# Splitting the weights in the DMA: high parts rounded by the load, low parts by a second, adding transfer

## The chip, the cores and the metric

The kernel runs on one core of a Trainium2 chip. TensorE (PE) multiplies, ScalarE (ACT) and VectorE (DVE) do the elementwise work, SyncE (SP) issues nearly all transfers, and GpSimd (POOL) has nothing to do but a few constants at the start. The metric is the device time of one execution in microseconds. Before the change three runs gave 1938.77, 1940.85 and 1942.29 us, a median of 1940.85 us.

## The reference

Two token streams share the weights: 128 context tokens and 512 latent tokens, 1024 channels each. Two layers follow each other. Layer 0 mixes tokens with a bidirectional state-space scan (the kernel calls it ssd), layer 1 with differential attention (att). Each is followed by a feed-forward block (ffn) with an up-projection, a depthwise convolution of width 3 and a down-projection:

```python
def conv_ffn(h, up_w, conv_w, conv_b, down_w):
    u = dwconv(h @ up_w, conv_w, conv_b)
    a, v = jnp.split(u, 2, axis=-1)
    return (jax.nn.silu(a) * v) @ down_w
...
        xp = xp + p_g1 * op
        xs = xs + s_g1 * os_
        ...
        xp = xp + p_g2 * conv_ffn(modulate(xp, norm_ffn_g[i], p_sh2, p_sc2), *ffn_p)
        xs = xs + s_g2 * conv_ffn(modulate(xs, norm_ffn_g[i], s_sh2, s_sc2), *ffn_p)
```

`modulate` is an RMS norm with a scale and a shift that come from a conditioning vector times a large matrix (`mod_w`). All inputs are float32, and the dense products are wanted at more than one reduced-precision pass gives.

## The kernel before, in words

Activations lie transposed: 128 channels on the partitions, 640 tokens along the row, 512 latent ones first. Every dense product is made in a split form. A float32 weight w is written as a high part (`whi`, rounded to the reduced type float32r) and a low part (`wlo` = w - whi, rounded to the same type), an activation likewise, and three products are summed: high by high, high by low, low by high. Each product is made in two matmuls of 256 and 384 tokens.

Weights are cut into 230 units. A unit is a tile of 128 partitions by up to 1024 columns, that is 8 blocks of 128x128 and 512 KB; it costs PE 8 x 3 x 2 = 48 matmuls. Units are numbered in the order of use: 0 is `w_dt`, 1 to 40 `w_in` (ssd), 41 to 56 `w_so`, 57 to 124 the first ffn (`w_up`, `w_dn`), then `w_qkv`, `w_ao` and the second ffn. `weight_units` lists them.

Three functions carry them. `prefetch` loads a unit into a raw tile (4 buffers) from SP's queue. `cast` makes the high part from the raw tile on ACT (line 134, a copy that rounds) and the low part on DVE (line 135, a subtraction); high and low have 3 buffers each, and in the two ffn stages two more of each for 2 units out of 5 (line 131). `nextw` hands out a unit, and keeps loads three units ahead of use and splits one unit ahead in program order (lines 141 and 142). A raw buffer comes free when DVE has subtracted from it, a high or low buffer when PE has read it for the last time.

The order of instructions on each engine is set by a scheduler from priorities and its own idea of durations. It may move a split further ahead than program order. At run time every engine and every queue works its list strictly in order, so an instruction that waits holds up all behind it. A queue also waits, before it issues a DMA, for the one eight issues earlier on it.

Beside the weights other things are loaded by SP: at the start the tokens (`xT`), constants and four blocks of the first modulation matrix (`modp`; tiles `mp`), later more of it (`mr`), and during the first ffn the second layer's modulation matrix in 48 tiles of 512 KB (`modT`; tiles `mw`, two buffers), which DVE reduces two instructions a tile (line 500). `hook`, called after each block of channels, advances such side tasks.

In the trace the up-projection's PSUM tiles are `up` (the first three of a stage `st`), the projections back to 1024 channels `po`, those of the ssd stage `in`, `x`, `bc`, `z`, those of attention `q`, `k`, `v`; `sl` are attention scores and `e` their exponentials; `uraw` is a copy of an `up` tile that ACT makes.

Of the kernel before, what the change touches and what calls it, by code (L numbers as in the profile page):

```python
# [9 lines left out]
F32 = mybir.dt.float32  # L10
F32R = mybir.dt.float32r
BF16 = mybir.dt.bfloat16
I32 = mybir.dt.int32
AF = mybir.ActivationFunctionType
ALU = mybir.AluOpType
# [3 lines left out]
P = 128  # L19
# [17 lines left out]
SUB = ((0, 8), (8, 15), (15, 22))  # L37
DA_SCALE = 64 ** -0.5
LAM_INIT = 0.8 - 0.6 * math.exp(-0.3 * 1)
RAW = 4  # L40
ATT_SPLIT = 6
NF = 19
RSQRT_MAGIC = float(0x5F3759DF)
# [2 lines left out]
class Step:  # L46
# [68 lines left out]


    def prefetch(self, upto):
        while len(self.wraw) <= min(upto, len(self.units) - 1):
            u = len(self.wraw)
            ap, n = self.units[u]  # L120
            r = self.pw.tile([P, 1024], F32, tag="raw", name=f"raw{u}", bufs=RAW)
            self.nc.sync.dma_start(r[:, :n], ap)
            self.wraw[u] = r

    def cast(self, upto):
        while len(self.wcast) <= min(upto, len(self.units) - 1):
            u = len(self.wcast)
            self.prefetch(u)
            n = self.units[u][1]
            r = self.wraw[u]  # L130
            wp, t, b = (self.pw, "w", 3) if self.px is None or u % 5 < 3 else (self.px, "x", 2)
            hi = wp.tile([P, 1024], F32R, tag=t + "hi", name=f"whi{u}", bufs=b)
            lo = wp.tile([P, 1024], F32R, tag=t + "lo", name=f"wlo{u}", bufs=b)
            self.act(hi[:, :n], r[:, :n], AF.Copy)
            self.tt(lo[:, :n], r[:, :n], hi[:, :n].bitcast(F32), ALU.subtract)
            self.wcast[u] = (hi, lo)

    def nextw(self):
        u = self.wi
        self.wi += 1  # L140
        self.prefetch(u + 3)
        self.cast(u + 1)
        return self.wcast[u]

    def dense(self, ps, w, ks, h):
# [332 lines left out]
    def mod_rest(self, l, t0, pool):  # L478


        nc, a = self.nc, self.a
        cb = pool.tile([P, 2, D], F32, tag="cbc", name="cbc", bufs=1)
        nc.sync.dma_start(cb, a["cbc"])
        for c in range(2):
            sb = self.pw.tile([P, 1024], F32, tag="raw", name="csil", bufs=RAW)
            self.act(sb, cb[:, c, :], AF.Tanh, scale=0.5)
            self.stt(cb[:, c, :], sb, 1.0, cb[:, c, :], ALU.add, ALU.mult)
            nc.vector.tensor_scalar(cb[:, c, :], cb[:, c, :], 0.5, None, ALU.mult)
        yield 4
        for t in range(t0 - 1, 48):  # L490
            if t < 47:
                nxt = pool.tile([P, 1024], F32, tag="mw", name="mw", bufs=2)
                nc.sync.dma_start(nxt, a["modT"][t + 1])
            if t < t0:
                w = nxt
                yield 8
                continue
            junk = self.slot("sq", "junk", BF16, cols=1024, bufs=1)
            for c in range(2):
                nc.vector.tensor_tensor_reduce(w if c else junk, w, cb[:, c, :], 1.0, 0.0, ALU.mult, ALU.add,  # L500
                                               self.mod[l][:, t, c:c + 1])
                yield 2 if self.down else 7
            if t % KT == KT - 1:
                for c in range(2):
                    mv = self.mod[l][:, t - KT + 1:t + 1, c]
                    self.tt(mv, mv, self.modb[:, 48 * l + t - KT + 1:48 * l + t + 1], ALU.add)
                if t // KT in (1, 4):
                    self.make_gs(l, t // KT // 3)
            w = nxt
# [590 lines left out]
    def run(self):  # L1100
        tc, nc, a = self.tc, self.nc, self.a
        self.units = self.weight_units()
        self.x = []

        def norm(l, s, h):
            def mk(hf):
                if hf == "A":
                    h.extend(self.new_h(f"h{l}{s}"))
                return self.norm_task(hf, self.gs[l][s], self.shift(l, s), h)
            return mk  # L1110

        hs = [[] for _ in range(4)]
        with tc.tile_pool(name="ssd", bufs=1) as pool:
            self.ssd(hs[0], norm(0, 1, hs[1]), pool)
        with tc.tile_pool(name="ffn0", bufs=1) as pool:
            self.px = pool
            self.modtask = self.add(self.mod_rest(1, 0, pool), 48)
            self.ffn(0, hs[1], norm(1, 0, hs[2]), pool)
            self.px = None
        with tc.tile_pool(name="att", bufs=1) as pool:  # L1120
            self.att_consts(pool)
            self.attention(hs[2], norm(1, 1, hs[3]), pool)
        with tc.tile_pool(name="ffn1", bufs=1) as pool:
            self.px = pool
            self.modtask = None
            self.ffn(1, hs[3], self.final_task, pool)
            for t in reversed(list(self.tasks)):
                self.drain(t)
# [100 lines left out]
```

## Time and profile before

| | |
|---|---|
| median of 3 runs | 1940.85 us (1938.77 to 1942.29) |
| the profiled execution's own time | 1941.6 us |
| its span, first to last instruction | 1939.8 us |
| granted TensorE clock, mean | 0.992 |
| instructions in the span | 33400 |
| bytes moved by DMA | 184.99 MB |

The span is what the profile covers; 1.8 us of the profiled execution lie around it. Busy times are unions of instruction records. Matmuls are pipelined and their ends modelled, so "PE busy" means that some matmul was in flight, not that PE ran at its peak. In the window table each engine has its busy time and its number of instructions, then come the granted clock, the mean busy share of the 16 DMA engines and the rate in GB/s. The chain of waits follows the work that ended last back to the start; a time on it for an engine other than PE is time in which PE's next matmul was held by that engine, or at least released by it last.

### The profile page before, as it was taken

How to read it: one execution, taken by the hardware profiler on the slowest of the kernel's cores; microseconds unless marked ns; L12 is line 12 of the kernel's file. 1: busy time of each engine (PE TensorE's matmuls, PEld its weight loads, DVE VectorE, ACT ScalarE, POOL GpSimd, SP SyncE). 2: the span in 40 equal slices, each digit the busy share in tenths (PEclk: the TensorE clock that was granted, in tenths of full speed). 3: DMA queues.
4: the chain of work that ended last, by engine and by line, in shares of the span. 5: the costliest groups of instructions: out<-in, count | busy, mean ns of one | idle time of the engine just before them, and what ended most of it. 6: DMA issues, size and time to landing. Idle time of an engine off the chain costs nothing.

```text
span 1939.8 us, 33400 instructions
## 1 busy us (share of the span) xinstructions
PE 1892.0 (98%) x13613; PEld 1785.8 (92%) x13613; DVE 1397.2 (72%) x2681; ACT 967.6 (50%) x1789; POOL 0.2 (0%) x4
## 2 busy tenths in 40 slices
PE   7999999999999999999999999999999999999997
PEld 4888888898988999999999988889899999999997
DVE  4779898888948999984455778888877553553554
ACT  2468585868633542243243576666645441441441
POOL 0000000000000000000000000000000000000000
PEclk8999999999999999999999999999999999999998
DMA  9611212113562456632222211111032222222211
GB/s 336 226 59 58 72 47 71 50 66 92 159 211 75 156 181 198 210 119 73 78 68 84 66 45 49 49 46 40 14 114 88 71 72 77 74 69 87 71 39 55
DMA packets 66729, 184.99 MB, mean 95 GB/s; under 512 B 8336, under 2 KB 14736, under 8 KB 66448
## 3 DMA queue, kind: packets, MB, share of 16 engines
q1 hardware_dynamic: 66000, 182.34, 29.1%
q8 instruction: 107, 1.75, 0.4%
q10 hardware_dynamic: 576, 0.52, 0.1%
q14 instruction: 46, 0.38, 0.1%
HBM read 177.06 MB, written 5.77 MB: 94 GB/s over the span
## 4 chain that ended last, share of the span: by engine, by line
PE 92%; ACT 3%; DVE 2%; DMA 1%; issue 1%; SPq 0%; DVEq 0%; ACTq 0%
PE up L102 30%; PE po L102 24%; PE z L102 6%; PE x L102 5%; PE st L102 4%; PE bc L102 3%; PE yp L102 3%; PE k L102 3%; PE q L102 3%; PE v L102 2%; PE sl L102 2%; PE ov L102 1%; PE modrow L102 1%; PE in L102 1%; PE wt L1007 1%; ACT e L93 1%
## 5 line engine op out<-in xcount | busy, mean ns | idle before, releaser
L93 ACT ACTIVATE whi<-raw 128x1024 fp32r<-128x1024 f32 (+4 forms) x230 | 236.1, 1027 | 410.0 <-PE po L102 232.3
L99 DVE TENSOR_TENSOR wlo<-raw,whi 128x1024 fp32r<-128x1024 f32 (+4 forms) x230 | 270.0, 1175 | 183.6 <-ACT whi L93 182.7
L96 DVE SCALAR_TENSOR_TENSOR xr<-po,mod,xr 128x256 f32<-128x256 f32 (+2 forms) x231 | 89.5, 433 | 162.3 <-PE po L102 162.1
L102 PE MATMUL po<-mh,whi 128*128 128x256 f32 (+1 forms) x704 | 167.6, 310 | 0.0
L102 PE MATMUL po<-ml,whi 128*128 128x256 f32 (+1 forms) x704 | 167.3, 310 | 0.0
L102 PE MATMUL po<-mh,wlo 128*128 128x256 f32 (+1 forms) x704 | 167.1, 309 | 0.0
L102 PE MATMUL up<-h01h,whi 128*128 128x256 f32 (+1 forms) x656 | 149.4, 308 | 0.7 <-ACT uraw L93 0.7
L102 PE MATMUL up<-h01h,wlo 128*128 128x256 f32 (+1 forms) x656 | 149.4, 308 | 0.0
L102 PE MATMUL up<-h11l,whi 128*128 128x256 f32 (+1 forms) x656 | 149.3, 308 | 0.0
L102 PE MATMUL up<-h11h,whi 128*128 128x256 f32 (+1 forms) x656 | 149.3, 308 | 0.0
L102 PE MATMUL up<-h11h,wlo 128*128 128x256 f32 (+1 forms) x656 | 149.3, 309 | 0.0
L102 PE MATMUL up<-h01l,whi 128*128 128x256 f32 (+1 forms) x656 | 149.3, 308 | 0.0
L102 PEld LDWEIGHTS po<-mh,whi 128*128 128x128 f32 x704 | 128.4, 188 | 0.6 <-ACT mh L93 0.4
L102 PEld LDWEIGHTS po<-mh,wlo 128*128 128x128 f32 x704 | 128.6, 188 | 0.0
L102 PEld LDWEIGHTS po<-ml,whi 128*128 128x128 f32 x704 | 128.4, 188 | 0.0
L102 PEld LDWEIGHTS up<-h01h,whi 128*128 128x128 f32 x656 | 119.2, 188 | 1.0 <-ACT uraw L93 1.0
L102 PEld LDWEIGHTS up<-h11h,wlo 128*128 128x128 f32 x656 | 119.3, 188 | 0.0
L102 PEld LDWEIGHTS up<-h11l,whi 128*128 128x128 f32 x656 | 119.3, 188 | 0.0
L102 PEld LDWEIGHTS up<-h01h,wlo 128*128 128x128 f32 x656 | 119.2, 188 | 0.0
L102 PEld LDWEIGHTS up<-h11h,whi 128*128 128x128 f32 x656 | 119.2, 188 | 0.0
L102 PEld LDWEIGHTS up<-h01l,whi 128*128 128x128 f32 x656 | 119.2, 188 | 0.0
L96 DVE SCALAR_TENSOR_TENSOR ca<-uraw,fcw,ca 128x127 f32<-128x127 f32 (+1 forms) x176 | 85.3, 545 | 11.4 <-ACT ca L93 11.4
(498 smaller groups left out, 4509.9 us busy)
## 6 DMA issues: line engine op xcount, KB each, us to landing
raw<-in_w_up SPq DMA_DIRECT2D x88, 512.0 KB, 3.5
mw<-in_modT SPq DMA_DIRECT2D x48, 512.0 KB, 3.6
raw<-in_w_in SPq DMA_DIRECT2D x40, 512.0 KB, 3.5
raw<-in_w_dn SPq DMA_DIRECT2D x32, 448.0 KB, 3.3
raw<-in_w_qkv SPq DMA_DIRECT2D x24, 512.0 KB, 3.5
mr<-in_mod SPq DMA_DIRECT2D x44, 256.0 KB, 5.0
raw<-in_w_so SPq DMA_DIRECT2D x16, 512.0 KB, 4.3
raw<-in_w_dn SPq DMA_DIRECT2D x16, 512.0 KB, 3.7
```

The source lines that it names most:

```text
L93: return self.nc.scalar.activation(out, in_, func, **k)
L96: return self.nc.vector.scalar_tensor_tensor(out, in0, s, in1, op0, op1)
L99: return self.nc.vector.tensor_tensor(out, a, b, op)
L102: return self.nc.tensor.matmul(out, lhsT, rhs, start=start, stop=stop)
L1007: nc.tensor.transpose(pm[:, b * P:(b + 1) * P], ws[b][:, kc * P:(kc + 1) * P], self.ident)
```

## The change

The changed kernel does not subtract on DVE. From unit 4 on:

- `prefetch` loads the unit straight into a high tile (float32r, 5 buffers) with a DMA from GpSimd's queue; the DMA converts float32 to float32r as it moves the bytes.
- `cast` lets ACT write the negated high part into the low tile (4 buffers), and then issues a second DMA from GpSimd's queue that reads the same weights again from memory and adds them to what stands in the low tile.
- The raw tiles remain for units 0 to 3 alone (4 buffers in the ssd stage's own pool), which are split on ACT and DVE as before.
- Splits are two units ahead of use in program order instead of one. The extra buffers of the ffn stages are gone.
- Two scratch tiles of the modulation (`csil`) use the `mw` tag instead of a raw buffer, and the descriptor ring for GpSimd's DMAs is 1024 bytes per partition instead of 256.

```diff
-RAW = 4
+FIRST = 4
...
     def prefetch(self, upto):
+
         while len(self.wraw) <= min(upto, len(self.units) - 1):
             u = len(self.wraw)
             ap, n = self.units[u]
-            r = self.pw.tile([P, 1024], F32, tag="raw", name=f"raw{u}", bufs=RAW)
-            self.nc.sync.dma_start(r[:, :n], ap)
+            if u < FIRST:
+                r = self.px.tile([P, 1024], F32, tag="raw", name=f"raw{u}", bufs=FIRST)
+                self.nc.sync.dma_start(r[:, :n], ap)
+            else:
+                r = self.pw.tile([P, 1024], F32R, tag="whi", name=f"whi{u}", bufs=5)
+                self.nc.gpsimd.dma_start(r[:, :n], ap)
             self.wraw[u] = r
 
     def cast(self, upto):
+
         while len(self.wcast) <= min(upto, len(self.units) - 1):
             u = len(self.wcast)
             self.prefetch(u)
-            n = self.units[u][1]
-            r = self.wraw[u]
-            wp, t, b = (self.pw, "w", 3) if self.px is None or u % 5 < 3 else (self.px, "x", 2)
-            hi = wp.tile([P, 1024], F32R, tag=t + "hi", name=f"whi{u}", bufs=b)
-            lo = wp.tile([P, 1024], F32R, tag=t + "lo", name=f"wlo{u}", bufs=b)
-            self.act(hi[:, :n], r[:, :n], AF.Copy)
-            self.tt(lo[:, :n], r[:, :n], hi[:, :n].bitcast(F32), ALU.subtract)
+            ap, n = self.units[u]
+            hi = self.wraw[u]
+            lo = self.pw.tile([P, 1024], F32R, tag="wlo", name=f"wlo{u}", bufs=4)
+            if u < FIRST:
+                r, hi = hi, self.pw.tile([P, 1024], F32R, tag="whi", name=f"whi{u}", bufs=5)
+                self.act(hi[:, :n], r[:, :n], AF.Copy)
+                self.tt(lo[:, :n], r[:, :n], hi[:, :n].bitcast(F32), ALU.subtract)
+            else:
+                self.act(lo[:, :n], hi[:, :n].bitcast(F32), AF.Copy, scale=-1.0)
+                self.nc.gpsimd.dma_start(lo[:, :n], ap, accum_op=ALU.add)
             self.wcast[u] = (hi, lo)
 
     def nextw(self):
         u = self.wi
         self.wi += 1
         self.prefetch(u + 3)
-        self.cast(u + 1)
+        self.cast(u + 2)
         return self.wcast[u]
...
-            sb = self.pw.tile([P, 1024], F32, tag="raw", name="csil", bufs=RAW)
+            sb = pool.tile([P, 1024], F32, tag="mw", name="csil", bufs=2)
...
-    nc = bacc.Bacc("TRN2", target_bir_lowering=False, num_devices=1, dynamic_dma_scratch_size=256)
+    nc = bacc.Bacc("TRN2", target_bir_lowering=False, num_devices=1, dynamic_dma_scratch_size=1024)
```

At the start of the program, on GpSimd's queue after the change (`whi4` is the high tile of unit 4): the loads of units 4 and 5 have nothing before them and no wait.

```order
L127 DMA whi4_447<-in_w_in 128x1024
L127 DMA whi5_449<-in_w_in 128x1024
L127 DMA whi6_708<-in_w_in 128x1024
L144 DMA wlo4_710<-in_w_in 128x1024
L144 DMA wlo5_713<-in_w_in 128x1024
L127 DMA whi7_827<-in_w_in 128x1024
```

Before, the same two units stood on SP's queue behind the tokens, the constants and the loads of all four modulation blocks; so two loads of 512 KB have moved to the front.

In the first ffn's up-projection, SP's queue before the change: the raw loads alternate with the modulation loads.

```order
L122 DMA raw70_7838<-in_w_up 128x1024
L493 DMA mw_8130<-in_modT 128x1024
L122 DMA raw71_7899<-in_w_up 128x1024
L493 DMA mw_8228<-in_modT 128x1024
L122 DMA raw72_7975<-in_w_up 128x1024
```

At the same place on GpSimd's queue after the change; the modulation loads stay on SP, alone.

```order
L127 DMA whi70_7777<-in_w_up 128x1024
L144 DMA wlo69_7779<-in_w_up 128x1024
L127 DMA whi71_7837<-in_w_up 128x1024
L144 DMA wlo70_7839<-in_w_up 128x1024
L127 DMA whi72_7912<-in_w_up 128x1024
L144 DMA wlo71_7914<-in_w_up 128x1024
```

One load per unit has become two, and each adding transfer stands directly behind the high load of the next unit.

On ACT at that place before the change (`up_7699` is the PSUM tile of unit 65, `up_7761` of unit 66): the rounding copy of unit 71 stands ahead of the evacuation of unit 66.

```order
L93 ACTIVATE uraw_7759<-up_7699 128x640
L93 ACTIVATE whi70_7977<-raw70_7838 128x1024
L93 ACTIVATE ca_7819<-uraw_7759,fcw0_7058 128x640
L93 ACTIVATE ca_7819<-ca_7819 128x640
L93 ACTIVATE whi71_8038<-raw71_7899 128x1024
L93 ACTIVATE uraw_7817<-up_7761 128x640
```

And after it (`up_7836` is unit 68): the negation of unit 72 follows the evacuation of unit 68.

```order
L93 ACTIVATE uraw_7834<-up_7776 128x640
L93 ACTIVATE wlo71_7914<-whi71_7837 128x1024
L93 ACTIVATE ca_7893<-uraw_7834,fcw0_7007 128x640
L93 ACTIVATE ca_7893<-ca_7893 128x640
L93 ACTIVATE uraw_7891<-up_7836 128x640
L93 ACTIVATE wlo72_7974<-whi72_7912 128x1024
```

ACT still has one 128x1024 instruction per unit, now later by about two units against PE, and it now waits for a landed high part instead of a landed raw tile.

More of the change, by code (lines that the diff above doesn't have):

```diff
@@ L1113, in run @@
         with tc.tile_pool(name="ssd", bufs=1) as pool:
+            self.px = pool
             self.ssd(hs[0], norm(0, 1, hs[1]), pool)
         with tc.tile_pool(name="ffn0", bufs=1) as pool:
-            self.px = pool
             self.modtask = self.add(self.mod_rest(1, 0, pool), 48)
             self.ffn(0, hs[1], norm(1, 0, hs[2]), pool)
-            self.px = None
         with tc.tile_pool(name="att", bufs=1) as pool:
@@ L1123, in run @@
         with tc.tile_pool(name="ffn1", bufs=1) as pool:
-            self.px = pool
             self.modtask = None
```

## The prediction

> **What bounds the kernel now.** I read the page's first and fourth part, then the table by stretches, then the waits of PE, then single tiles.
>
> ```profile
> PE 1892.0 (98%) x13613; PEld 1785.8 (92%) x13613; DVE 1397.2 (72%) x2681; ACT 967.6 (50%) x1789; POOL 0.2 (0%) x4
> PE 92%; ACT 3%; DVE 2%; DMA 1%; issue 1%; SPq 0%; DVEq 0%; ACTq 0%
> ```
>
> PE has matmuls in flight for 98% of the span and carries 92% of the chain. Only 47.8 us (1939.8 - 1892.0) are free of matmuls, so a change that gives PE nothing less to do has little to win.
>
> ```profile
> 0.00:30.00 30.00, 19.99 (x221) 8.43 (x222) 13.18 (x27) 10.06 (x16) 0.20 (x4) 0.89 0.97 354
> 120.00:240.00 120.00, 119.57 (x932) 106.25 (x930) 106.55 (x212) 85.89 (x214) 0.00 (x0) 1.00 0.18 62
> 240.00:350.00 110.00, 108.42 (x869) 96.41 (x868) 97.55 (x196) 78.14 (x194) 0.00 (x0) 1.00 0.19 63
> 636.00:741.00 105.00, 105.00 (x717) 105.00 (x716) 104.04 (x179) 52.62 (x66) 0.00 (x0) 1.00 0.53 174
> 741.00:797.00 56.00, 56.00 (x391) 56.00 (x390) 55.57 (x100) 11.76 (x13) 0.00 (x0) 1.00 0.70 214
> 797.00:895.00 98.00, 98.00 (x669) 98.00 (x668) 77.62 (x133) 42.37 (x54) 0.00 (x0) 1.00 0.42 128
> 1090.00:1175.00 85.00, 79.02 (x492) 72.30 (x491) 71.32 (x149) 58.00 (x118) 0.00 (x0) 0.98 0.14 43
> 1175.00:1380.00 205.00, 198.80 (x1309) 182.40 (x1308) 172.50 (x341) 139.98 (x286) 0.00 (x0) 1.00 0.14 45
> 1380.00:1457.00 77.00, 73.15 (x537) 68.13 (x536) 56.57 (x126) 36.36 (x66) 0.00 (x0) 1.00 0.25 78
> 1477.00:1583.00 106.00, 106.00 (x725) 106.00 (x724) 64.67 (x100) 53.81 (x66) 0.00 (x0) 1.00 0.27 85
> 1583.00:1639.00 56.00, 56.00 (x384) 56.00 (x383) 20.68 (x35) 10.43 (x12) 0.00 (x0) 1.00 0.23 76
> 1639.00:1738.00 99.00, 99.00 (x677) 99.00 (x676) 52.72 (x81) 44.09 (x54) 0.00 (x0) 1.00 0.23 70
> ```
>
> After length and busy times come clock, DMA share and GB/s. Four things are to be seen. The start is bound by transfers: 354 GB/s with the DMA engines 97% busy. In both ffn blocks (rows from 636 and from 1477) PE is never idle, although DVE is full in the first (104.04 of 105) and half empty in the second: the DVE time of the split costs nothing there. Attention (rows from 1090 to 1457) has 6.0 + 6.2 + 3.85 = 16.0 us without matmuls, the ssd stage 0.4 and 1.6 us in its two rows. And the first ffn already moves twice the bytes of the second, since `modT` is loaded beside the weights.
>
> ```profile
> PE sl L102 <- ACT e L93: 6.6, 7, 2.1
> PE q L102 <- ACT e L93: 5.6, 6, 1.1
> PE po L102 <- DVE wlo L99: 0.6, 1, 0.6
> ```
>
> These are PE's waits (total, times, longest). 12.2 us of attention's 16.0 wait for ACT's exponentials, and the subtraction on DVE, which the change takes away, holds PE for 0.6 us in the whole run.
>
> **The change part by part.** The sums are against the profiled execution (1941.6 us); the median is 0.75 us below it.
>
> *DVE loses the subtraction.*
>
> ```profile
> L93 ACT ACTIVATE whi<-raw 128x1024 fp32r<-128x1024 f32 (+4 forms) x230 | 236.1, 1027 | 410.0 <-PE po L102 232.3
> L99 DVE TENSOR_TENSOR wlo<-raw,whi 128x1024 fp32r<-128x1024 f32 (+4 forms) x230 | 270.0, 1175 | 183.6 <-ACT whi L93 182.7
> L93 ACT ACTIVATE ca<-uraw,fcw x44: 907/922/928, 635.7 to 1866.3; 128x640 f32<-128x640 f32 x44
> ```
>
> 226 of 230 go: 265 us of DVE. What reaches the end is at most the idle of PE that DVE causes. In the ssd rows that is at most 2.0 us; I take 1.0, since PE's waits name other tiles too. In attention it is 16.0 at most and, without the waits for ACT, 16.0 - 12.2 = 3.8; I take 3.8, because ACT keeps its load. Term: -4.8, bounds 0 and -18.
>
> *ACT rounds no more, it negates.* One 128x1024 instruction per unit takes the place of another. A copy costs 1027 ns, about 1.0 ns a column; `ca`, which has a scale and a bias, 922 ns for 640 columns, 1.44 a column. The negation has a constant scale and no bias, so it is nearest to the copy: 0, bounds 0 and +0.4 us a unit, which ACT's idle half covers except in attention (40 units, +16 us at worst).
>
> *Two loads of 512 KB move to the front.* The chain at the start:
>
> ```profile
> 5.16 5.91 DMA x<-in_xT
> 11.09 4.35 DMA mp<-in_modp
> 15.46 8.04 DMA mp1x<-in_modp
> 29.46 7.27 PE in L102 x36
> ```
>
> PE's first dense product waits for transfers that come one after another at 354 GB/s. Units 4 and 5 now share the engines with them from the first microsecond: 1.05 MB / 354 GB/s = 3.0 us later. They were not needed before 68 us. Term: +3.0; bounds 0 (they fall into gaps) and +3.0.
>
> *The low part is a second DMA.* Its queue, its latency and its bytes are to be priced.
>
> ```profile
> 635.26 105.92 PE up L102 x720
> raw<-in_w_up SPq DMA_DIRECT2D x88, 512.0 KB, 3.5
> L122 SPq DMA_DIRECT2D raw<-in_w_up x88: 327/328/463, 558.1 to 1810.7; - x88
> ```
>
> 720 matmuls are 15 units, 7.06 us each. GpSimd's queue gets two DMAs a unit. The trace of before shows no issue from there; SP's take 0.33 us, and even ten times that fits (6.6 of 7.06 us). Term 0.
>
> Latency: by the order lists the negation of unit 71 follows the evacuation of unit 67, that is about the start of unit 68. Three units, 21.2 us, remain for evacuation (0.7), negation (1.0) and the adding transfer. A plain load lands in 3.5 us; five times that would still do. The high load of unit 72 is issued when PE is through with unit 67 and its negation comes one unit later: 7.06 against 3.5 us. If it is late, ACT stands there with the evacuation of unit 69 behind it, and PE goes on into two further PSUM buffers. Term 0.
>
> Bytes: let the adding transfer cost the DMA engines as much as k plain loads. The rate wanted is then the row's own plus k times the weights' part, which the second ffn shows alone (85, 76, 70 GB/s). In the first ffn that is 174 + 85k, 214 + 76k, 128 + 70k, in the second 85 + 85k, against 354 at best. No row has an adding transfer. Below, k = 1: it writes what a load writes. Above, I carry k = 4. It must read the weights and also what stands in the low tile, so I take 2: 344, 366, 268, 255. Only the stretch from 741 to 797 is over, by 12/354 of 56 us. Term: +1.9, bounds 0 and, with k = 4, some +170 (below).
>
> The Trainium skill (Collectives: The Full Stack, on the bandwidth ceiling and the fold count) has a price: a reduce in the DMA runs at half the rate of a copy because of its two reads, not because of the add; by it the term would be the same +1.9, and no run here shows it yet.
>
> Sum: 1941.6 - 4.8 + 0 + 3.0 + 1.9 = 1941.7, against the median 1941.
>
> **The rivals.** *A: the adding transfer is dear (slower).* Place: GpSimd's DMAs in both ffn blocks. It decides from k = (354 - 85)/85 = 3.2, where the second ffn's rate is over the ceiling. At k = 4 the second ffn wants 425: 20% of its 395 us (1477 to 1872) is +79; the first wants 514, 518 and 408: 0.45 x 105 + 0.46 x 56 + 0.15 x 98 = 88, together about +170, 2110 us; at k = 6 (595, and 684, 670, 548) it is 0.68 x 395 + 0.93 x 105 + 0.89 x 56 + 0.55 x 98 = 470, 2410 us. For it: nothing in the trace shows a transfer that reads its own destination. Against it: 16 engines have 73% of their time free in the second ffn.
>
> *B: the first ffn alone is overfull, k from 2.2 to 3.2 (slower).* At k = 3: 429 and 442 GB/s, 0.21 x 105 + 0.25 x 56 = 36 us of transfers too many, less the 19 us of lead of the low parts: about +17, with the start's 3 some 1960. Or the `mw` loads get late and DVE, in order, holds the evacuations behind its reduction.
>
> *C: more relief than the waits name (faster).* PE's idle in attention is ACT's, but ACT's inputs come from a DVE that is 84% busy (172.50 of 205) and loses a seventh. All 16 us would go: 1941.6 - 16 - 2 + 3 = 1927. Against it: 12.2 us are put down to ACT.
>
> *D: GpSimd is held up while it prepares its DMAs (slower).* DVE has instructions in its fast two-port form:
>
> ```profile
> L936 DVE CAST kl<-kl x16: 487/488/491, 1115.0 to 1369.8; 64x640 fp32r<-64x640 f32 x16
> L488 DVE TENSOR_SCALAR cbc<-cbc x2: 686/688/689, 609.8 to 611.9; 128x1024 f32<-128x1024 f32 x2
> ```
>
> Both run below 0.8 ns a column where the subtraction needs 1.15. These 18 instructions together are 9.2 us, one at most 0.7 us against the 19 us of lead: if all of it came through, 1950. The rule is in the Trainium skill (SBUF — State Buffer, the box on the trap that DVE blocks DMA): a copy or `tensor_scalar` in a two-port mode keeps GpSimd from writing descriptors. The trace of before has no DMA of GpSimd's, so it can't say.
>
> **How the numbers follow.** 0.2% is 3.9 us, about what a measurement of this kernel tells from no change. The forecast (cover holds, k about 2) has 0.46, its own range 1930 to 1948 from the bounds of its terms, and splits into 0.21 faster, 0.15 same, 0.10 slower. A has 0.24: a price without a row may be anywhere. B 0.14, C 0.10, D 0.06. Faster is 0.21 + 0.10 = 0.31, same 0.15, slower 0.10 + 0.24 + 0.14 + 0.06 = 0.54. The range: below it 0.05 are left out by ending at 1927, a little under C; above, half of A, 0.12, by ending at 2060 (k about 3.6).
>
> **What the profile after would show.** DVE's `wlo` group with 4 instructions and busy time near 1130 us; ACT's group `wlo<-whi` with 226 of about 1.03 us; GpSimd's queue with 452 DMAs; `x720` of `up` still in 105.9 us. The time from issue to landing of the adding DMA is the test: under 10 us and a DMA share below 0.95 after 636 us speak for the forecast; a share near 1, and PE waiting for `wlo` by DMA in the second ffn, for A; the same in the first alone for B. The first `in` matmul should start near 32.5 instead of 29.46 us. Attention's three rows should lose about 4 us of idle, 16 by C. The prediction is wrong if a unit of `up` takes more than 7.1 us, or if ACT's negation waits on landing high parts long enough to hold PSUM.

## The result and the profile after

Four runs of the changed kernel gave 1988.87 to 1994.05 us, a median of 1989.21 us, against 1941.57 us for four of the kernel before: a ratio of 1.0253, with a 95% interval of 1.0233 to 1.0273. The change costs 2.5%. The profiled execution of after has a span of 1987.5 us (before 1939.8), so there are 47.7 us to find.

The page of after, in the order busy time (first part), queues (third) and chain (fourth):

```profile
PE 1901.6 (96%) x13613; PEld 1796.6 (90%) x13613; DVE 1159.7 (58%) x2455; ACT 958.7 (48%) x1789; POOL 323.4 (16%) x456
...
q0 software_dynamic: 65088, 227.57, 53.7%
q1 hardware_dynamic: 33456, 68.55, 9.9%
...
PE 69%; issue 12%; DMA 6%; DVE 3%; POOL 2%; ACT 2%; POOLq 0%; DVEq 0%; ACTq 0%
```

DVE is busy for 237 us less (the 226 records that went add up to 265; neighbouring records overlap, and busy time is their union), ACT kept its load, and PE's share of the chain fell from 92 to 69%. GpSimd's queue (q0) alone now keeps the 16 DMA engines busy for 53.7% of the span.

Where the time went is read by position in PE's work and not by clock time: the start of every 32nd matmul that reads a high part, in PE's order, in both traces, and the growth of the difference from one such mark to the next. The columns of experiments are explained further down. Stages that a run leaves alone still differ from after: the 112 us of the first ffn lose 27.5 to 33.2 us in such runs, the first edge 7.3 to 10.8, the start 2.3 to 3.7. Differences of that size are not read as an effect.

| stage (time in before, us) | after | plain low load | short modulation loads | loads spread | more modulation buffers | no modulation loads | more weight tiles | both |
|---|---|---|---|---|---|---|---|---|
| start, to 68 | +3.5 | +3.0 | +3.7 | +2.4 | +2.5 | +3.1 | +3.4 | +2.9 |
| ssd, 68 to 596 | +6.5 | +0.1 | +5.5 | +7.2 | +5.0 | +8.4 | +6.9 | +8.2 |
| first ffn until 720 | +1.3 | -1.6 | +3.8 | +0.9 | +3.1 | +1.5 | +0.8 | +2.2 |
| first ffn, 720 to 832 | **+28.2** | +9.3 | +15.7 | +30.9 | +2.2 | -0.4 | +33.2 | +2.2 |
| first ffn, 832 to 1058 | -2.4 | -2.4 | -0.2 | -2.4 | -2.4 | -0.2 | -0.2 | -2.4 |
| edge to attention, 1058 to 1131 | **+7.6** | +6.1 | +10.4 | +8.6 | +7.7 | +8.9 | +0.3 | +1.3 |
| attention, 1131 to 1428 | -5.7 | -6.7 | -5.7 | -5.4 | -5.1 | -5.3 | -7.4 | -7.5 |
| edge to the second ffn, to 1462 | **+10.3** | +5.2 | +9.9 | +8.7 | +7.6 | +8.0 | +3.5 | +2.5 |
| second ffn | -1.5 | -1.4 | -1.7 | -1.8 | -1.7 | -1.4 | -1.8 | -1.7 |
| sum | +47.7 | +11.6 | +41.4 | +49.2 | +18.8 | +22.7 | +38.8 | +7.8 |

More than half of the loss lies in 112 us of the first ffn. The same work of PE there before and after:

```profile
720.00:832.00 112.00, 112.00 (x772) 112.00 (x771) 110.90 (x197) 34.12 (x40) 0.00 (x0) 1.00 0.65 202
```

```profile
731.00:871.00 140.00, 122.04 (x770) 119.55 (x769) 98.82 (x190) 38.53 (x47) 25.25 (x35) 0.94 0.84 225
```

PE stands idle for 18.0 us more, and its matmuls take 10.0 us longer. The second part is the granted clock: the trace has it at 0.50 in four spells, from 763.8, 791.1, 815.0 and 849.1 us, 17.1 us in all, each beside one of PE's stops, and before has no such spell between 624 and 1119 us. Half of 17.1 us, 8.5 us, is at most lost by it. A pair of matmuls within a spell stands below against one outside:

```profile
768.80 0.45 PE L102 MATMUL po<-mh,whi 128*128 128x256 f32 x2
...
792.16 0.88 PE L102 MATMUL po<-mh,whi 128*128 128x256 f32 x2 [3.12 <-issue]
```

The table by stretches of after (length; busy time and count of PE, PEld, DVE, ACT, POOL; clock, DMA share, GB/s), in that place and in the same work of the second ffn:

```profile
731.00:752.00 21.00, 18.94 (x127) 18.34 (x126) 17.47 (x34) 8.45 (x11) 4.31 (x6) 1.00 0.92 241
752.00:769.00 17.00, 14.48 (x89) 13.96 (x88) 15.79 (x30) 6.17 (x8) 2.88 (x4) 0.90 0.80 233
769.00:796.00 27.00, 22.39 (x140) 21.93 (x139) 19.87 (x38) 7.95 (x9) 6.00 (x9) 0.91 0.97 260
...
1526.00:1632.00 106.00, 106.00 (x725) 106.00 (x724) 45.17 (x83) 51.83 (x64) 22.32 (x31) 1.00 0.78 164
```

The second ffn has weights of the same size, the same adding transfers and a DMA share of 0.78, and PE is never idle in it. In the first PE is idle by the microsecond, while the transfers are under way for 80 to 97% of the time. DVE, which was full here before (110.90 of 112 us), now has room and still stops. Why is in the waits (total, times, longest), first of before from 720 to 832, then of after from 731 to 870:

```profile
ACT mh L93 <- DVE cv L99: 15.3, 4, 5.2
ACT ca L93 <- DVE ca L96: 12.5, 4, 3.7
...
DVE junk L500 <- DMA mw<-in_modT: 0.5, 1, 0.5
```

```profile
POOL wlo L144 <- ACT wlo L93: 81.8, 18, 10.4
...
DVE junk L509 <- DMA mw<-in_modT: 31.6, 13, 6.3
ACT ca L93 <- DVE ca L96: 28.5, 5, 13.5
...
ACT mh L93 <- DVE cv L99: 27.1, 5, 7.2
ACT wlo L93 <- DMA whi<-in_w_dn: 11.8, 3, 5.6
```

and, row by row, in ACT's part of the timeline there (start, duration; in brackets the idle time before and what ended it):

```profile
744.18 0.74 ACT L93 ACTIVATE mh<-cv 128x640 fp32r<-128x640 f32 x1 [4.46 <-DVE cv L99]
...
753.07 0.74 ACT L93 ACTIVATE ca<-ca 128x640 f32<-128x640 f32 x1 [5.80 <-DVE ca L96]
...
762.22 0.74 ACT L93 ACTIVATE mh<-cv 128x640 fp32r<-128x640 f32 x1 [6.07 <-DVE cv L99]
```

DVE waits 31.6 us for modulation slices (`mw`), and in order everything else of DVE's stands behind them. ACT waits for the gate's instructions (28.5 and 27.1 us, before 12.5 and 15.3), with the next negation behind them, and GpSimd's queue waits for the negation (81.8 us). That last wait is the largest, but hardly what PE pays for: the second ffn has 76.6 us of it, too (1526 to 1922 us), and PE is never idle there. PE itself is held by a shorter way. A `po` tile is one of three PSUM buffers, and DVE evacuates it (`xr`). In DVE's part of the timeline, ahead of the stop of 3.12 us shown above:

```profile
789.78 1.23 DVE L509 CUSTOM_DVE_ANT_0 junk<-mw,cbc 128x1024 bf16<-128x1024 f32 x1 [4.69 <-DMA mw<-in_modT]
...
790.93 1.13 DVE L96 SCALAR_TENSOR_TENSOR xr<-po,mod,xr 128x256 f32<-128x256 f32 x3
```

DVE waited 4.69 us for a slice, made its product, then evacuated `po` until 792.06, and PE went on at 792.16. The profile names no releaser for most of these stops ("issue"), but six of them, 13.4 of the 18.0 us, end 0.10 us after such an evacuation, three directly behind a product that had waited 4.6 to 6.3 us for its slice; at the end of the longest one (5.0 us, until 814.85) both parts of the unit's weights had been there for over 10 us. Weights that came late hold PE for some 2 us here, the gate's `mh` and `ml` for 2.5. The modulation slices land later beside GpSimd's transfers; issue to landing, median, of after:

```profile
whi<-in_w_up POOLq DMA_DIRECT2D x88, 512.0 KB, 3.8
wlo<-in_w_up POOLq DMA_DIRECT2D x88, 512.0 KB, 5.9
mw<-in_modT SPq DMA_DIRECT2D x48, 512.0 KB, 5.6
```

A slice landed in 3.6 us before (median of all; 4.1 in this stretch), and in 4.4 us in the run with plain low loads below. In the down-projection DVE is to take one about every 3.5 us (two products, one every two of PE's steps of 7.06 / 8 = 0.88 us), and there are two buffers: before, the next slice was just there (DVE waited once, 0.5 us), and with a landing time of 5.6 us it isn't. That is a reading so far; the runs below try it.

### The profile page after: what moved, and what is told of

Same layout as the page of the kernel before. It is cut to its first block, busy times and chain, and to the rows that moved or that the text cites. A ratio compares the mean times of both kernels' runs of the same rounds, so it can differ in the third digit from the quotient of the medians.

```text
span 1987.5 us, 33670 instructions
## 1 busy us (share of the span) xinstructions
PE 1901.6 (96%) x13613; PEld 1796.6 (90%) x13613; DVE 1159.7 (58%) x2455; ACT 958.7 (48%) x1789; POOL 323.4 (16%) x456
## 3 DMA queue, kind: packets, MB, share of 16 engines
q0 software_dynamic: 65088, 227.57, 53.7%
## 4 chain that ended last, share of the span: by engine, by line
PE 69%; issue 12%; DMA 6%; DVE 3%; POOL 2%; ACT 2%; POOLq 0%; DVEq 0%; ACTq 0%
PE up L102 24%; PE po L102 16%; PE z L102 6%; DMA mw<-in_modT 3%; PE x L102 3%; PE yp L102 3%; PE k L102 3%; PE q L102 2%; PE bc L102 2%; PE v L102 2%; PE st L102 2%; PE sl L102 2%; POOL wlo L144 1%; PE ov L102 1%; POOL whi L127 1%
## 5 line engine op out<-in xcount | busy, mean ns | idle before, releaser
L93 ACT ACTIVATE wlo<-whi 128x1024 fp32r<-128x1024 f32 (+3 forms) x226 | 232.3, 1028 | 288.9 <-PE po L102 246.1
L96 DVE SCALAR_TENSOR_TENSOR cv<-uraw,fcw,cv 128x511 f32<-128x511 f32 (+1 forms) x176 | 85.2, 546 | 166.5 <-ACT cv L93 166.5
L96 DVE SCALAR_TENSOR_TENSOR ca<-uraw,fcw,ca 128x511 f32<-128x511 f32 (+1 forms) x176 | 85.2, 547 | 107.3 <-ACT ca L93 107.3
L102 PEld LDWEIGHTS po<-mh,whi 128*128 128x128 f32 x704 | 129.1, 191 | 14.4 <-issue 10.3
```

What stands on the lines that cost most here:

```text
L93: return self.nc.scalar.activation(out, in_, func, **k)
L96: return self.nc.vector.scalar_tensor_tensor(out, in0, s, in1, op0, op1)
L102: return self.nc.tensor.matmul(out, lhsT, rhs, start=start, stop=stop)
```

## The experiments

All are changed kernels but the last two. Each single time stands beside a run of the kernel before on the same chip (1941.82 us for the first four, 1940.44 for the next four; the last four stand beside 23 runs with a median of 1939.55 us). Theories are numbered anew in the second set.

### Is it the adding?

```diff
-                self.nc.gpsimd.dma_start(lo[:, :n], ap, accum_op=ALU.add)
+                self.nc.gpsimd.dma_start(lo[:, :n], ap)
```

> The second transfer of each unit loads the weights over the low tile without adding, so the low parts are wrong (they are the rounded weights); everything else is as in the changed kernel. Theory 1 (bytes: the 16 DMA engines are overfull in the first ffn because an adding transfer costs about two plain loads): the share of GpSimd's queue falls from 53.7% to about 35%, the 28 us lost between 731 and 871 us shrink to under 8, the time is near 1967 us. Theory 2 (latency and order: load, negation and second transfer stand in three in-order queues, whatever they move): the loss there stays above 20 and the time stays near 1987 us.

Measured: 1953.13 us; 36 of the 47.7 us go. The price of the addition comes from the second ffn, where PE waits for nothing. The stretch of the up-projection in this run, whose row in after is the last one above:

```profile
1489.00:1594.00 105.00, 105.00 (x717) 105.00 (x716) 46.05 (x84) 52.09 (x65) 16.39 (x31) 1.00 0.56 165
```

Two plain loads a unit are a DMA share of 0.56, one so 0.28; with the addition it is 0.78, so the adding transfer takes 0.50, that is k = 0.50 / 0.28 = 1.8 plain loads. The Trainium skill (Collectives: The Full Stack, on the fold count) has a reduce at half the rate of a copy, because it reads two sources; the page says so of rings of several cores. Carried over to this transfer, k would be 2; the trace is near that. GpSimd also issues for longer with it: 323.4 against 239.5 us in all. That ssd loses nothing here (+0.1 for +6.5) makes the adding transfers its cause too, though not by which wait.

### Is it the modulation's bytes?

46 of 48 modulation slices cut to 64 of 1024 columns:

```diff
+        keep = [pool.tile([P, 1024], F32, tag="mw", name="mw", bufs=2) for _ in range(2)]
...
-                nxt = pool.tile([P, 1024], F32, tag="mw", name="mw", bufs=2)
-                nc.sync.dma_start(nxt, a["modT"][t + 1])
+                nxt = keep[(t + 1) % 2]
+                m = 1024 if t < 1 else 64
+                nc.sync.dma_start(nxt[:, :m], a["modT"][t + 1, :, :m])
```

Both products of a slice are written to the scratch tile `junk` here, as in the run without modulation loads.

> The second layer's modulation loads bring 64 of 1024 columns from the third tile on (the modulation is then wrong), so 46 of the 48 loads of 512 KB are cut to a sixteenth; DVE's reductions stay. Theory 1 (bytes): the loss of 28 us in the first ffn goes to under 3, the time is near 1962 us. Theory 2 (order of GpSimd, ACT and DVE alone): the loss stays above 20, the time near 1987 us.

Measured: 1983.24 us. The first ffn still loses 15.7 us, although its DMA share is only 0.67: the bytes can't be the whole of it. The slices of 32 KB take 4.3 us to land (median, 740 to 830 us), and DVE still waits for them (20.1 us in 7 times, up to 6.1).

### Is it their bunching?

```diff
-                yield 2 if self.down else 7
+                yield 5
```

> The modulation steps come every 5 hooks through the whole first ffn instead of every 7 in the up-projections and every 2 in the down-projections; the same bytes, spread over some 440 instead of 240 us. Theory 1 (bytes at the same time): the loss of 28 us falls to 3 to 10, the time is 1964 to 1972 us. Theory 2 (order): 1985 to 1992 us.

Measured: 1991.01 us, no gain. DVE waits as long as in after (35.9 us between 731 and 870).

### Are three units at a time too many for the tiles?

At both edges three units are used side by side. Here those ahead of the edges get low tiles of their own, and the 256-column units of `w_ao` small tiles:

```diff
+        if tag == "wlo" and u in (122, 123, 124, 159, 160, 161) or tag == "whi" and u in ():
+            pool, tag, bufs = self.px, "x" + tag, 3
+        elif u in (154, 155, 156, 157, 158):
+            pool, tag, bufs, cols = self.px, "s" + tag, 4, 256
```

> The low tiles of the last three units of the first ffn and of attention get buffers of their own (3 more low tiles in those two stages), and the five short units of the attention output (256 columns) get 4 high and 4 low tiles of their own. Theory 3 (at the two stage ends three units are used at once and the next three find no low tile free, so that load, negation and adding transfer are waited for): the 7 us lost at the end of the first ffn go to under 3 and the 11 us at the end of attention to under 5, the time is near 1977 us. Rival (bytes there too): no change, 1989 us.

Measured: 1998.30 us, 9 us worse. By the marks, with the small high tiles (`swhi`) counted among the high parts, the first edge loses 14.5 instead of 7.6 us, attention loses 1.7 instead of gaining 5.7, the first ffn loses 32.5, and only the second edge is free (-1.8 instead of +10.3). Low tiles at these units alone are no cure; why it got worse was not followed.

### Buffers for the modulation

```diff
-                nxt = pool.tile([P, 1024], F32, tag="mw", name="mw", bufs=2)
+                nxt = pool.tile([P, 1024], F32, tag="mw", name="mw", bufs=5)
...
-                yield 2 if self.down else 7
+                yield 5
```

> The changed kernel, its modulation loads given five buffers instead of two and one slice's product asked for every five steps of PE's loop instead of every two (or seven). Theory 1 (in the first ffn VectorE, in order, is held by modulation loads that take 5.6 instead of 3.5 us with only one buffer ahead, and with it the gates and evacuations that ScalarE's negations stand behind): the loss of 28 us there falls under 10, and the time to about 1968. Theory 2 (the queues are simply full: adding transfer and loads together need more than there is): more buffers change nothing, 1985 to 1992.

Measured: 1960.68 us. The first ffn loses 2.2 us instead of 28.2, the rest stays. DVE no longer waits for a slice in its products at all. The rows of this run that answer to the three of after:

```profile
731.00:752.00 21.00, 21.00 (x146) 21.00 (x145) 20.96 (x40) 9.38 (x12) 4.00 (x7) 1.00 1.02 300
752.00:769.00 17.00, 17.00 (x115) 17.00 (x114) 16.86 (x32) 5.84 (x7) 3.98 (x7) 1.00 1.03 283
769.00:796.00 27.00, 27.00 (x182) 27.00 (x181) 26.76 (x55) 4.12 (x4) 5.18 (x8) 1.00 0.99 293
```

The DMA engines are completely busy for 65 us, and slices land later than in after (6.8 us, median), yet PE is never idle, and the clock is 1.00. So neither the bytes nor a full set of DMA engines was what PE paid for; it was that DVE stood still. Spreading alone had brought nothing, so the buffers are needed; whether they do it alone wasn't run.

### No modulation loads at all

```diff
+        keep = pool.tile([P, 1024], F32, tag="mw", name="mw", bufs=2)
+        nc.sync.dma_start(keep, a["modT"][0])
...
-                nxt = pool.tile([P, 1024], F32, tag="mw", name="mw", bufs=2)
-                nc.sync.dma_start(nxt, a["modT"][t + 1])
+                nxt = keep
```

> The changed kernel with 47 of the 48 modulation loads left out: VectorE makes all 96 products from the first slice, without a wait (the second layer's modulation comes out wrong). Theory 1 (VectorE held by late loads): the first ffn loses 0 to 5 us instead of 28, 1961 to 1967. Theory 3 (the order alone: a low part's transfer can't be asked for before ScalarE's negation, the next high part's transfer stands behind it on GpSimd's queue, and ScalarE stands behind a VectorE that is full of products): some 16 us stay, as they did with short loads, 1976 to 1984.

Measured: 1964.11 us, first ffn -0.4 us. With all of DVE's work and ACT's order in place the loss is gone once the wait is. The bytes of 47 slices are gone here too, but the run with five buffers had kept those. The rival, order alone, falls. Over the runs DVE's wait for slices from 600 to 870 us and the loss between 720 and 832 go roughly together: 56.1 and 33.2 (more weight tiles, the next run), 52.2 and 30.9 (spread), 47.3 and 28.2 (after), 29.4 and 9.3 (plain low load), 23.8 and 15.7 (short loads), none and 2.2 (more modulation buffers), none and -0.4 (no loads). The plain low load falls out of that line.

### Weight tiles

```diff
-                r = self.pw.tile([P, 1024], F32R, tag="whi", name=f"whi{u}", bufs=5)
+                r = self.pw.tile([P, 1024], F32R, tag="whi", name=f"whi{u}", bufs=6)
...
-            lo = self.pw.tile([P, 1024], F32R, tag="wlo", name=f"wlo{u}", bufs=4)
+            lo = self.pw.tile([P, 1024], F32R, tag="wlo", name=f"wlo{u}", bufs=5)
```

> The changed kernel with six buffers for high parts and five for low parts instead of five and four (the room comes from one of the four first raw tiles). Theory 4 (where three units are in use at once, GpSimd's queue stands 19 us behind a high part that waits for a buffer, and the low parts behind it): the edges' losses of 7.6 and 10.3 us and the ssd stage's 6.5 fall by half or more, together 10 to 18 us, 1971 to 1979. Rival (the latency of two transfers in a row, which no buffer shortens): within 4 us of 1989.

Measured: 1980.18 us. The edges lose 0.3 and 3.5 instead of 7.6 and 10.3 us; ssd is unmoved (+6.9), and so, within its spread, is the first ffn (+33.2): tiles for the weights were not what it lacked. PE's waits for weights, in after over the whole run:

```profile
PE st L102 <- DMA wlo<-in_w_qkv: 6.0, 1, 6.0
...
PE po L102 <- DMA wlo<-in_w_ao: 5.0, 3, 3.4
...
PE st L102 <- DMA wlo<-in_w_up: 4.9, 2, 2.5
```

and with six and five tiles:

```profile
POOL whi L127 <- PE st L102: 55.1, 3, 25.8
...
PE po L102 <- DMA wlo<-in_w_ao: 3.4, 3, 1.7
```

In after a low part at an edge came up to 6.0 us after PE wanted it. GpSimd's queue still stands up to 25.8 us behind a high tile that PE's `st` products hold, but one more unit of each kind is then already there. Here too a part of the loss is clock: in after it stands at 0.50 for 10.2 us at each edge, before for 3.4 us at the first and not at all at the second, so at most 3.4 and 5.1 us of the two losses.

### The start

```diff
-FIRST = 4
+FIRST = 6
```

(with four raw buffers as before)

> The changed kernel with six instead of four units loaded raw by SyncE's queue. If the 3.4 us at the start are GpSimd's first two loads and two adding transfers in the burst of the start, as the forecast's term of 3.0 had it, the start falls back to within 1 us of before, and the time to about 1986. If the burst itself (its bytes) is the cause, the 3.4 us stay: 1989.

Measured: 1989.56 us. The start loses 2.0 instead of 3.5 us. Runs that leave the start alone lose 2.3 to 3.7, so hardly any of the loss is shown to be these two units' own, and most of it stayed.

### Both cures

Four modulation buffers with one product every five steps, and six high and five low tiles.

> The changed kernel with both cures: four modulation buffers and one product every five steps, six high and five low tiles. If the two losses are separate, the 27 us of the first ffn and some 13 us of the edges go together: 1989 - 27 - 13 = 1949, 1945 to 1953; what stays over before is the start (3), the ssd stage (6 to 7) less attention's gain. If they are one loss that shows at two places, only the larger cure counts: about 1960.

Measured: median 1949.74 us of four runs, 1.0055 times the time of before (1.0040 to 1.0070, 23 runs of it). The two losses are separate. What is left over before by the table is the start (2.9) and ssd (8.2) with smaller ones, less attention's 7.5.

### Attention's gain: VectorE's relief?

```diff
+                if 125 <= u < 149:
+                    j = self.pc.tile([P, 1024], F32R, tag="jk", name="jk", bufs=1)
+                    self.tt(j[:, :n], hi[:, :n].bitcast(F32), hi[:, :n].bitcast(F32), ALU.subtract)
```

> The changed kernel with one VectorE subtraction of 128x1024 given back to each of the units 125 to 148 (from the high part to a tile that nobody reads). If attention's gain of 5.7 us is VectorE's relief (the forecast's term of 3.8), the stretch from 1131 to 1428 us of before gains at most 2 us; if it comes from ScalarE's earlier negation or the extra unit of lead, it still gains 4 to 6.

Measured: 2006.02 us; attention loses 6.8 us instead of gaining 5.7. The table by stretches, attention of after and of this run:

```profile
1176.00:1467.00 291.00, 284.09 (x1869) 260.75 (x1868) 216.02 (x456) 190.42 (x384) 38.86 (x55) 1.00 0.40 84
```

```profile
1181.00:1485.00 304.00, 291.34 (x1873) 261.47 (x1873) 235.00 (x474) 191.60 (x387) 39.10 (x55) 1.00 0.39 81
```

and the waits of this run:

```profile
DVE jk L99 <- DMA whi<-in_w_qkv: 10.9, 12, 2.9
```

19 us more of DVE's work make it 12.5 us longer, so attention does hang on DVE although PE's waits mostly name ACT. The size is not a fair price of the subtraction: the added one waits on DVE for landing high parts, which the old one didn't.

### The adding transfer in attention alone

The kernel before with the new scheme for units 128 to 148, and a control without. Both have four raw, four high and four low tiles and none of the extra tiles of the ffn stages.

```diff
+def ADDS(u):
+    return 128 <= u < 149
...
+            if ADDS(u):
+                hi = r
+                self.act(lo[:, :n], hi[:, :n].bitcast(F32), AF.Copy, scale=-1.0)
+                self.nc.gpsimd.dma_start(lo[:, :n], ap, accum_op=ALU.add)
```

> The kernel before with the adding transfer for the units 128 to 148 of attention alone (four raw, four high, four low tiles throughout, cast two units ahead for those units only). If attention's gain is the change's own and the losses are the other stages', 3 to 6 us are gained: 1935 to 1938. If the gain is given back at the end of the stage, where its units are released together, 1940 to 1943.

> The control for the run beside it: the kernel before with four raw, four high and four low tiles throughout and no adding transfer. Theory: tiles alone move nothing, 1939 to 1943.

Measured: 1938.85 us (0.9998, 0.9989 to 1.0008) with it and 1936.68 us (0.9991, 0.9981 to 1.0001) without; neither can be told from before. By the marks the adding run pays 4.3 us at the edge where the scheme begins and gets nothing back in attention (-0.1), the control -0.3 and -0.4. So attention's gain doesn't stand by itself with four tiles of each kind. Nothing tried here beats the kernel before. The hybrid with six and five tiles wasn't tried.

## Why the prediction was right or wrong

The sum said no change, 1941.7 us, and was 47 us too low; the range, 1927 to 2060, and the larger chance, 0.54 for slower, held what came. That the range held is luck as far as the mechanism goes: it reached 2060 for the sake of rival A, a dear adding transfer, and that is not what happened. What happened was in rival B, with a chance of 0.14. By its own steps:

- **DVE loses the subtraction, -4.8.** Right in kind. Attention gains 5.7 us in after and up to 7.5 with enough buffers, against 3.8 put down; ssd's 1.0 can't be seen under that stage's loss. The reading that PE's 12.2 us behind ACT's exponentials would stay, because ACT keeps its load, was wrong: by the waits of after they are 0.3 (`sl`), 3.5 (`q`) and, new, 1.9 us (`k`), so about half went. That this half had been DVE's at one remove, which was rival C's mechanism, is shown in part: with the subtraction given back `sl` returns to 3.3 us, but `q` stays at 3.5. The gain is a third of C's 16 us. The stretch of before that answers to attention's row above has 12.2 us without matmuls (after 6.9):

```profile
1131.00:1428.00 297.00, 284.78 (x1869) 260.73 (x1868) 241.17 (x485) 192.44 (x389) 0.00 (x0) 1.00 0.14 43
```

- **ACT negates, 0.** Right: 226 negations of 1028 ns on average, a copy had 1027.

```profile
L93 ACT ACTIVATE wlo<-whi 128x1024 fp32r<-128x1024 f32 (+3 forms) x226 | 232.3, 1028 | 288.9 <-PE po L102 246.1
```

- **Two loads at the front, +3.0.** The first `in` matmul starts at 31.8 us (first number of the tile's row below, behind the durations) instead of 29.46; 32.5 was forecast, and the loss up to 68 us is 3.5. The size fits, but the reason isn't shown: giving the two units back to SP's queue left a loss of 2.0, hardly less than other runs have.

```profile
L102 PE MATMUL in<-h00h,whi x48: 277/332/522, 31.8 to 60.9; 128*128 128x256 f32 x16, 128*128 128x384 f32 x16, 128*64 128x256 f32 x8, 128*64 128x384 f32 x8
```

- **Issue, 0.** Right. The adding issues took 853 to 899 ns in the ffn and 853 to 888 in attention, two per unit far below 7 us:

```profile
L144 POOL DMA_DIRECT2D wlo<-in_w_up x88: 853/869/899, 592.4 to 1894.5; - x88
...
L144 POOL DMA_DIRECT2D wlo<-in_w_qkv x24: 853/870/888, 1099.3 to 1367.1; - x24
```

  The `kl` casts of rival D run in attention as well, and the median there is the same, with one issue for `w_ao` of 1114 ns as the longest: no sign of GpSimd being held up. The rule of the Trainium skill (SBUF — State Buffer, the box on the trap that DVE blocks DMA) isn't seen at so few instructions.
- **Bytes, +1.9, from k = 2.** k is 1.8, and the consequence drawn for the second ffn (never idle) is right. Even where the engines were completely busy, from 731 to 796 us with more buffers, PE lost nothing. Rivals A and, in its first form, B are out.
- **Latency, 0. This is the step that failed.** It followed a unit's own two transfers, found three units of lead and stopped there; what other loads wait for was put at nothing. It failed twice. First, what else is on the DMA engines got later: modulation slices from 3.6 to 5.6 us, with two buffers and DVE waiting in order, and PE waited for the PSUM tiles that DVE evacuates behind its products. That is rival B's second sentence, mechanism and all, which had a place but no price, and a chance of 0.14 together with the first; it cost 28.2 of the 47.7 us, up to 8.5 of them in matmuls at half the clock, which no term had. The forecast had quoted the row that pointed there: DVE was full (55.57 of 56 us). Its own sign of being wrong named PSUM held by ACT's negation; PSUM was held, but by DVE. Secondly, the three units of lead were read from the middle of the up-projection. At the stage edges, where three units are used side by side, five high and four low tiles don't give them: 7.6 and 10.3 us, of which one more tile of each kind took 14.1 away.
- **Not forecast at all:** ssd, +6.5 against -1.0. It goes with the plain low load (+0.1) and stays with every other cure. In the waits of after, ACT and DVE stand behind the store of the state:

```profile
ACT h L93 <- DMA out_st<-h: 5.0, 4, 2.3
...
DVE h L99 <- DMA h<-in_h: 4.7, 1, 4.7
...
DVE h L99 <- DMA out_st<-h: 4.1, 1, 4.1
```

  Before, 0.6 us of waiting for `out_st` was all. The loss would fit these waits, but with the plain low load 5.0 us of the 9.1 behind `out_st` remain and the stage loses nothing. After also has two spells of 3.4 us at a granted clock of 0.50 here, from 139.1 and 453.2 us, where before has none; at most 3.4 us come from them. No run took the waits away, so the cause stays open.

## What to carry to other kernels

A transfer that relieves one engine can be paid for by whatever else is in flight, here by 28 of 48 us. List every other load and store by the time it takes to land against the buffers that cover it, not only the new transfer by its own lead. An engine that works in order is the place where a late load does its harm: PE waited for none of the late slices itself, it waited for the evacuations that stood behind them. The longest wait in a list need not be the one that counts; look at what ended just before the bottleneck engine went on. In this kernel a full set of DMA engines did no harm once the late consumer had buffers enough, and the lead had to be counted at the edges of stages, not in their middle.

## What was not expected of the hardware

Beside the transfers from GpSimd's queue those of SP's queue landed later even where the DMA engines were on average far from full: in ssd (60 to 610 us; DMA share 0.49 between 120 and 240 us, before 0.18) the loads of the state, `h`, took 8.3 instead of 4.0 us to land, and the modulation rows `mr` 8.2 instead of 4.9. With plain low loads they took 4.9 and 6.5. And slices of 32 KB still took 4.3 us in the first ffn, against 5.6 for 512 KB: most of the time to land was not their own bytes. And a stop of PE could cost more than its own length: the stop of 5.0 us until 814.85 was followed by 3.4 us at a granted clock of 0.50, while the one of 1.5 us until 781.63 was not.
